# Splitting the input weights once and reading the parts back from device memory

## The chip, the cores and the metric

The kernel runs on one core of one Trainium2 chip. The core has a matrix engine (TensorE, PE in the profile, with its weight loads as PEld), three engines for elementwise work (VectorE or DVE, ScalarE or ACT, GpSimd or POOL), a queue that issues all of this kernel's transfers (SyncE or SP), and 16 DMA engines that move the bytes between device memory and the on-chip buffers. The metric is the device time of one execution in microseconds; less is better.

## The reference: one step of a streaming encoder layer

The input is 2048 new frames of one stream (1024 wide), 16 learned meta tokens ahead of them, and 32 further frames of a second, running stream with a cache of 16 + 512 keys and values. In short:

```
n = rmsnorm(x, norm_g)                       # 1024 wide
q, k, v, z_a, b, c, u, z_c = split(n @ w_in) # w_in is 1024 x 4096, eight parts of 512
for 4 heads (q, k in two halves of 64):      # keys visible up to the query's chunk of 64
    a = softmax(q1 k1/8 + bias) - lambda * softmax(q2 k2/8 + bias)
    o = 0.8 * rmsnorm(a @ v, subln_g) * silu(z_a)
y_c = silu(z_c) * b * conv3(c * u)           # causal, depthwise, width 3
y = rmsnorm(x + concat(o, y_c) @ w_out)
```

Outputs are y for both streams, the new keys and values, and the last two rows of the convolution's input. Everything is float32.

## The kernel before

**Products in three parts.** TensorE is fed with numbers of a rounded float32 kind (F32R). To keep float32's accuracy each operand is cut in two: a high part, which is the operand rounded by a cast, and a low part, which is the operand minus the high part. A product is then three: high x high, high x low, low x high. In `proj` these are the three matmuls of line 212 for each of eight slices of the 1024 inputs.

**Blocks and units.** The new frames go in four blocks of 512 tokens (`p` = 0 to 3); block 0 also carries the meta tokens and the 32 frames of the second stream, 560 columns in all. The normalised input of a block stays on chip, transposed, as eight pairs of high and low slices (`xh`, `xl`, from `x_load`). For each block the loop at line 725 goes over four heads. `unit_a(h, p)` projects keys, values, queries and gate of one head: four tiles of 128 columns of `w_in`. `attend` scores the queries against all keys so far (lines 428 and 429, 16 to 2064 of them), takes the softmax of both halves (lines 375 to 383) and multiplies with the values (lines 444 to 461). `unit_c(u, p)` does one 128-channel tile of the convolution: four more tiles of `w_in`. So each block goes through all 32 column tiles of `w_in`, 128 tile visits in all. Afterwards lines 740 to 743 do the output projection (line 676) and the final norm for 17 tiles of tokens.

**A weight tile.** `w_load(col, p)` brings one tile of 128 columns (1024 x 128, 512 KB) into a staging tile `wr`, of which there are two. It then handles it in two halves of 512 inputs: ScalarE casts the half to its high part `wh` (line 191), and GpSimd, or VectorE for a few tiles, subtracts to get the low part `wl` (line 192). There are four buffers for `wh` and four for `wl`, so two whole tiles can stand ready. In block 0 each matmul group runs twice, over two column ranges of about 280 tokens; in later blocks once, over 512: 48 and 24 matmuls for a tile. The same 32 tiles are loaded and cut again in each of the four blocks.

**Keys and queries around an attention.** The scores need the high part of a half head's keys in partitions 0 to 63 and the low part in 64 to 127. So the parts of new keys (`kh`, `kl`, lines 235 and 236) and queries (`qh`, `ql`, lines 313 and 314) are moved across partitions by transfers: eight for q, four for new ks. Earlier keys and values are kept in device memory (`ksd`, `vd`) and read back in each later block: four transfers for ks, two for v. There is one buffer of `ks` and of `q`, so these transfers start when the attention before has read its own. The bias tile `bz` has one buffer too.

**What sets the order.** The program names engines and tiles; a planner with a simulated clock puts all instructions of an engine in one order at build time, and each engine, and SP with the transfers, keeps that order at run time. A buffer is handed on when every instruction that reads it has ended. All transfers go through SP (the helper at line 73), so one that must wait holds those behind it.

**The output projection's input.** `load_cat` (line 643) reads a tile of the concatenated result into the same staging buffers as `wr` and cuts it in two into the same buffers as `wh` and `wl`.

Of the kernel before, what the change touches and what calls it, by code (L numbers as in the profile page):

```python
# [11 lines left out]
F32 = mybir.dt.float32  # L12
F32R = mybir.dt.float32r
AF = mybir.ActivationFunctionType
ALU = mybir.AluOpType
AX = mybir.AxisListType

P = 128
D = 1024
KT = D // P  # L20
# [9 lines left out]
EPS = 1e-6  # L30
# [17 lines left out]
def hybrid_step(ctx: ExitStack, tc: tile.TileContext, x, xT, ckT, cv, scT, rel_bias, norm_g, w_in,  # L48
# [28 lines left out]

# [1 line left out]
    ident = const.tile([P, P], F32, name="ident")  # L79
# [16 lines left out]

# [1 line left out]
    xh, xl = {}, {}  # L98
    rbs = {}

    def x_stats(p):
        """1 / rms of each token, in the token's partition."""
        ssq = sm.tile([P, 8], F32, tag="ssq", name="ssq", bufs=1)
        for j in range(8):
            xr = one.tile([P, QT], F32, tag="xt", name="xr", bufs=XB)
            r0 = NX + QT * p + P * (j // 2)
            dma(xr, x[r0:r0 + P, 512 * (j % 2):512 * (j % 2) + 512])
            S.activation(xr, xr, AF.Square, accum_out=ssq[:, j:j + 1])
        ssp, var, r, w = (sm.tile([P, 4], F32, tag=f"x{i}", name=f"x{i}", bufs=1) for i in range(4))
        V.tensor_reduce(ssp, ssq.rearrange("p (t i) -> p t i", i=2), op=ALU.add, axis=AX.X)  # L110
        rsqrt(r, ssp, var, w, 1.0 / D)
        return r

    def x_rms(p, r):
        """rb[:, t] = 1 / rms of token t, the same in every partition."""
        rb = one.tile([P, NX + QT], F32, tag="rb", name="rb")
        pb = ps_j.tile([P, 512], F32, tag="pj", name="pb")
        dg = one.tile([P, QT], F32, tag="xt", name="dg", bufs=XB)
        with tc.high_priority():
            V.tensor_tensor(by_tile(dg), ident.unsqueeze(1).broadcast_to([P, 4, P]),  # L120
                            r.unsqueeze(2).broadcast_to([P, 4, P]), op=ALU.mult)
            T.matmul(pb, lhsT=ones, rhs=dg, start=True, stop=True)
            S.copy(rb[:, :QT], pb)
        rbs[p] = rb
# [38 lines left out]
    def rsqrt(r, ssum, var, w, scale):  # L163
        """r = 1/sqrt(scale * ssum + EPS), with one Newton step on the table's value."""
        V.tensor_scalar(var, ssum, scale, EPS, op0=ALU.mult, op1=ALU.add)
        S.activation(r, var, AF.Ln)
        S.activation(r, r, AF.Exp, scale=-0.5)
        V.tensor_tensor(w, r, r, op=ALU.mult)
        V.tensor_tensor(w, w, var, op=ALU.mult)
        V.tensor_scalar(w, w, -0.5, 1.5, op0=ALU.mult, op1=ALU.add)  # L170
        V.tensor_tensor(r, r, w, op=ALU.mult)

    def softplus_neg(out, z):
        """log(1 + exp(-z)) for any z: beyond 40 it equals -z in float32."""
        V.tensor_scalar(out, z, -1.0, 40.0, op0=ALU.mult, op1=ALU.min)
        S.activation(out, out, AF.Exp)
        S.activation(out, out, AF.Ln, bias=1.0)
        V.scalar_tensor_tensor(out, z, -1.0, out, op0=ALU.mult, op1=ALU.max)

# [1 line left out]
    pre = {}  # L181

    def w_load(col, p):
        wr = wp.tile([P, KT, P], F32, tag="wraw", name="wr")
        dma(wr, w_in[col])
        w2 = []
        for i in range(2):
            wh = wp.tile([P, KT // 2, P], F32R, tag="wh", name="wh", bufs=4)
            wl = wp.tile([P, KT // 2, P], F32R, tag="wl", name="wl", bufs=4)
            wi = wr[:, KT // 2 * i:KT // 2 * (i + 1)]  # L190
            S.copy(wh, wi)  # L191
            (V if (col in (CK, CV) if p == 0 else col in (CQ, CZ)) else G).tensor_tensor(wl, wi, f32(wh), op=ALU.subtract)  # L192
            w2.append((wh, wl))
        return w2
# [20 lines left out]

# [1 line left out]
    ksd = [dram.tile([2, P, NK], F32, name=f"ksd{h}", tag=f"ksd{h}") for h in range(H)]  # L217
# [121 lines left out]

# [1 line left out]
    def coefs(nm, l, nch, pn, lam=None):  # L341
        """nm, l: [pn, components, nch] negated maxima and sums; returns the factor of each (component, chunk)."""
        n = nm.shape[1]
# [18 lines left out]
    def softmax_diff(pn, chunks, mm, bz):  # L362
        """chunks: [(first column, width)]; mm(c, ps, col, w) writes negated scores, bz is the negated bias of the
        last 512 columns; returns the chunks of a."""
        nch = len(chunks)
# [20 lines left out]
    def chunks_of(t):  # L386
        """The columns (16 meta, then t + 1 tiles of 128) in pieces of at most 512, cut between tiles."""
        n = t + 1
        g = -(-(NM + P * n) // 512)
        cuts = [n * j // g for j in range(g + 1)]  # L390
        cols = [0] + [NM + P * c for c in cuts[1:]]
        return [(cols[j], cols[j + 1] - cols[j]) for j in range(g)]
# [73 lines left out]
    def attend_sample(h, st):  # L466
        """Rows 0..31: component 0 of the queries; rows 32..63: component 1."""
        kts, cvt, q2, (z32, l1) = st["kts"], st["cvt"], st["qs"], st["z"]
# [38 lines left out]

# [1 line left out]
    def unit_c(u, p):  # L509
# [54 lines left out]

# [1 line left out]
    bvs, bzd = [], []  # L566
# [22 lines left out]
    def prep_small():  # L589
# [18 lines left out]
        S.activation(ls, ls, AF.Exp)  # L608
        # (1, -lambda) / sg and EPS / sg^2 with sg = max(1, |lambda|): the head norm keeps its value, and its range.
        sg = const.tile([P, 2], F32, name="sg")  # L610
# [11 lines left out]

# [1 line left out]
    y0 = [dram.tile([P, 512], F32, name=f"y0_{t}", tag=f"y0_{t}") for t in range(17)]  # L624
# [18 lines left out]
    def load_cat(t, rows, spare=False):  # L643
# [3 lines left out]
        for i in range(2):  # L647
            c = ct[:, 4 * i:4 * i + 4, :rows]
            if spare:
                chh, cll = [pp.tile([P, 4, P], F32R, tag="p0", name="cs", bufs=NP[0]) for _ in range(2)]  # L650
            else:
                chh = wp.tile([P, 4, P], F32R, tag="wh", name="chh", bufs=4)
                cll = wp.tile([P, 4, P], F32R, tag="wl", name="cll", bufs=4) if t < 16 else chh
            S.copy(chh[:, :, :rows], c)  # L654
# [6 lines left out]
    def half_product(y, c, w, rows, ssq):  # L661
        """y (the residual) += cat @ w for 512 columns, and the sum of its squares."""
        chh, cll = c
# [52 lines left out]

# [1 line left out]
    after = (((0,), (1,), (2, 3), ()), ((0,), (1,), (2,), (3,)))  # L718
# [74 lines left out]
```

## Time and profile before

| | |
|---|---|
| Time, median of 3 runs | 1342.75 us (1339.35 to 1343.84) |
| Profiled execution, its span from first to last instruction | 1338.5 us |
| TensorE matmuls busy | 1285.5 us, 96% of the span |
| VectorE, ScalarE, GpSimd busy | 999.3, 717.6, 682.8 us |
| DMA: bytes, mean rate | 215.59 MB, 161 GB/s |
| Weight loads from `w_in` | 128 of 512 KB |

The profile is of one execution, and its times are in us from the first instruction. "Busy" is the time in which an engine's own instructions run; matmuls are pipelined, so a busy TensorE is not one at its peak. A row of a group reads: line, engine, operation, out<-in, shapes, count, busy us, mean ns of one, then the engine's idle time just before these instructions and what ended it. A row of waits reads: who waited, for whom, us in total, how often, the longest. In the table by stage each row has the stretch, its length, then busy us and count for PE, PEld, DVE, ACT and POOL, the granted TensorE clock, the share of the 16 DMA engines and GB/s. The time of a transfer to its landing runs from its issue on SP.

### The profile page before, as it was taken

Reading aid. Unit: us, or ns where it says so; the run is one execution under the profiler, and the core shown is the slowest. Engines: PE = TensorE matmul, PEld = TensorE weight load, DVE = VectorE, ACT = ScalarE, POOL = GpSimd, SP = SyncE. Lnnn points to the kernel's source line nnn. Section 1 sums busy time; section 2 is a strip of 40 time slices with the busy share of each in tenths; the row PEclk is TensorE's granted clock in tenths of the full one; section 3 lists DMA queues with packets and bytes.
Section 4 is the critical chain, followed back from the end, with each engine's and each line's share of the span. In section 5 each row is a group of like instructions: output and inputs, shape, how many; then the busy total and the mean of one; then the engine's idle time right before and its main releaser. Section 6 shows DMA issues by size and latency. Waiting matters only on the chain.

```text
span 1338.5 us, 21190 instructions
## 1 busy us (share of the span) xinstructions
PE 1285.5 (96%) x7058; PEld 1104.2 (82%) x7058; DVE 999.3 (75%) x2086; ACT 717.6 (54%) x1814; POOL 682.8 (51%) x619
## 2 busy tenths in 40 slices
PE   8899999999999999999999999998999999999997
PEld 6899999977878878878878788887887877878875
DVE  8677676668887958788888898786785895777753
ACT  5554454555564547454645566465554665674432
POOL 4555556455555663565566535564574573452200
PEclk9999999999999999999999999999999999999999
DMA  8754543894445377545453463636247348445851
GB/s 276 229 155 125 164 117 104 245 274 138 139 147 158 103 209 232 141 151 150 150 135 126 120 208 93 167 124 143 94 110 203 117 160 215 165 150 185 273 196 52
DMA packets 118670, 215.59 MB, mean 161 GB/s; under 512 B 19840, under 2 KB 48032, under 8 KB 118560
## 3 DMA queue, kind: packets, MB, share of 16 engines
q1 hardware_dynamic: 118560, 214.23, 54.7%
q8 instruction: 56, 0.92, 0.3%
q14 instruction: 54, 0.44, 0.1%
HBM read 145.62 MB, written 43.26 MB: 141 GB/s over the span
## 4 chain that ended last, share of the span: by engine, by line
PE 59%; DVE 16%; DMA 10%; issue 4%; ACT 4%; POOL 3%; SPq 2%; DVEq 0%; POOLq 0%; ACTq 0%
PE pj L212 37%; PE po L676 6%; DVE p L383 3%; PE s L428 3%; DMA q<-r 3%; PE s L429 3%; PE pt L444 3%; SPq L73 2%; DVE nm L378 2%; PE po L452 2%; PE po L453 2%; PE po L451 2%; DMA ks<-ksd 1%; ACT p L379 1%; POOL wl L192 1%
## 5 line engine op out<-in xcount | busy, mean ns | idle before, releaser
L212 PE MATMUL pj<-xh,wh 128*128 128x512 f32 (+2 forms) x1280 | 457.0, 358 | 4.0 <-ACT wh L191 1.3
L192 POOL TENSOR_TENSOR wl<-wr,wh 128x512 fp32r<-128x512 f32 x240 | 328.7, 1375 | 250.2 <-ACT wh L191 234.7
L212 PE MATMUL pj<-xl,wh 128*128 128x512 f32 (+2 forms) x1280 | 455.1, 356 | 0.8 <-DVE xl L140 0.8
L212 PE MATMUL pj<-xh,wl 128*128 128x512 f32 (+2 forms) x1280 | 454.7, 356 | 0.0
L379 ACT ACTIVATE p<-s,nm 128x384 f32<-128x384 f32 (+5 forms) x352 | 208.8, 595 | 186.8 <-DVE nm L378 135.1
L212 PEld LDWEIGHTS pj<-xh,wh 128*128 128x128 f32 x1280 | 243.2, 190 | 34.2 <-ACT bvec L586 2.0
L212 PEld LDWEIGHTS pj<-xh,wl 128*128 128x128 f32 x1280 | 242.9, 190 | 31.2 <-issue 1.3
L212 PEld LDWEIGHTS pj<-xl,wh 128*128 128x128 f32 x1280 | 243.4, 190 | 30.1 <-DVE xl L140 1.4
L191 ACT CAST wh<-wr 128x512 fp32r<-128x512 f32 x256 | 157.0, 616 | 129.4 <-PE pj L212 78.6
L383 DVE SCALAR_TENSOR_TENSOR p<-p,cf,p 128x384 f32<-128x384 f32 (+5 forms) x176 | 174.5, 1019 | 28.1 <-POOL p L382 27.8
L428 PE MATMUL s<-ks,q 128*128 128x384 f32 (+5 forms) x352 | 129.5, 375 | 26.8 <-DMA q<-r 10.0
L382 POOL TENSOR_SCALAR p<-p,cf 128x384 f32<-128x384 f32 (+5 forms) x176 | 125.0, 726 | 49.2 <-DVE cf L359 35.1
L378 DVE TENSOR_REDUCE nm<-s 128x1 f32<-128x400 f32 (+3 forms) x224 | 122.5, 557 | 28.2 <-PE s L429 27.9
L429 PE MATMUL s<-ks,q 128*128 128x384 f32 (+5 forms) x352 | 124.0, 354 | 2.0 <-DMA q<-r 2.0
L448 DVE TENSOR_TENSOR al<-pt,ah 128x512 fp32r<-128x512 f32 x144 | 97.0, 682 | 37.0 <-ACT ah L447 36.9
L656 POOL TENSOR_TENSOR cll<-ct,chh 128x512 fp32r<-128x512 f32 x40 | 53.9, 1353 | 113.6 <-ACT chh L654 105.4
L428 PEld LDWEIGHTS s<-ks,q 128*128 128x128 f32 x352 | 66.2, 190 | 42.5 <-issue 14.4
L447 ACT CAST ah<-pt 128x512 fp32r<-128x512 f32 x144 | 79.1, 585 | 40.8 <-PE pt L444 40.7
L375 DVE CUSTOM_DVE_ANT_0 s<-s,bz 128x512 f32<-128x512 f32 (+5 forms) x128 | 74.4, 585 | 17.9 <-PE s L429 13.5
L444 PE MATMUL pt<-ident,p 128*128 128x128 f32 x544 | 86.5, 274 | 0.0
L452 PE MATMUL po<-al,vh 128*128 128x256 f32 x288 | 84.2, 292 | 1.9 <-DVE al L448 1.7
L451 PE MATMUL po<-ah,vh 128*128 128x256 f32 x288 | 81.6, 283 | 0.0
(243 smaller groups left out, 2138.4 us busy)
## 6 DMA issues: line engine op xcount, KB each, us to landing
wr<-in_w_in SPq DMA_DIRECT2D x128, 512.0 KB, 4.1
q<-r SPq DMA_DIRECT2D x128, 128.0 KB, 4.7
ct<-cat SPq DMA_DIRECT2D x28, 512.0 KB, 4.8
out<-y SPq DMA_DIRECT2D x32, 256.0 KB, 3.4
ks<-ksd SPq DMA_DIRECT2D x16, 388.0 KB, 7.8
xr<-in_x SPq DMA_DIRECT2D x24, 256.0 KB, 4.8
out<-g SPq DMA_DIRECT2D x24, 256.0 KB, 4.5
xt<-in_xT SPq DMA_DIRECT2D x24, 256.0 KB, 4.2
```

Source lines behind the costliest of these rows:

```text
L191: S.copy(wh, wi)
L192: (V if (col in (CK, CV) if p == 0 else col in (CQ, CZ)) else G).tensor_tensor(wl, wi, f32(wh), op=ALU.subtract)
L212: T.matmul(ps, lhsT=a[:, k % 4], rhs=b[k][:, b0:b1], start=(k == 0 and i == 0), stop=(k == KT - 1 and i == 2))
L378: V.tensor_reduce(nm[:, c, j:j + 1], s, op=ALU.min, axis=AX.X)
L379: S.activation(pr[j][c], s, AF.Exp, bias=nm[:, c, j:j + 1], scale=-1.0, accum_out=l[:, c, j:j + 1])
L382: G.tensor_scalar(a0, a0, cf[:, 0, j:j + 1], 1.0, op0=ALU.mult, op1=ALU.mult)
L383: V.scalar_tensor_tensor(a0, a1, cf[:, 1, j:j + 1], a0, op0=ALU.mult, op1=ALU.add)
L428: T.matmul(ps, lhsT=qd[c][0][:, qs], rhs=ks[c][:, col:col + w], start=True, stop=False)
L429: T.matmul(ps, lhsT=qd[c][1][:, qs], rhs=ks[c][:, col:col + w], start=False, stop=True)
L444: T.transpose(pt[:, i, P * qi:P * (qi + 1)], cols(aa[qi], NM + P * (2 * j + i), P), ident)
L451: T.matmul(po, lhsT=vh[:, kt], rhs=ah[:, i], start=(kt == 0), stop=False)
L452: T.matmul(po, lhsT=vh[:, kt], rhs=al[:, i], start=False, stop=False)
```

## The change

In block 0 a weight tile is loaded and cut as before, but the two parts of a half lie side by side in one buffer (`w2`, four buffers of twice the size), and each half is also stored to device memory, high and low part together, 512 KB a half. In blocks 1 to 3 nothing is staged or cut: each half comes with one load of 512 KB from there straight into a `w2` buffer, two loads for a tile where there was one. The choice of VectorE or GpSimd for the subtraction is that of block 0. `load_cat` takes its two parts from one `w2` buffer. Comments and docstrings are taken out as well; they are left out here.

```diff
+    wd = [dram.tile([P, 2, 2, KT // 2, P], F32, name=f"wd{c}", tag=f"wd{c}") for c in range(32)]
+
     def w_load(col, p):
-        wr = wp.tile([P, KT, P], F32, tag="wraw", name="wr")
-        dma(wr, w_in[col])
+
+        if p == 0:
+            wr = wp.tile([P, KT, P], F32, tag="wraw", name="wr")
+            dma(wr, w_in[col])
         w2 = []
         for i in range(2):
-            wh = wp.tile([P, KT // 2, P], F32R, tag="wh", name="wh", bufs=4)
-            wl = wp.tile([P, KT // 2, P], F32R, tag="wl", name="wl", bufs=4)
-            wi = wr[:, KT // 2 * i:KT // 2 * (i + 1)]
-            S.copy(wh, wi)
-            (V if (col in (CK, CV) if p == 0 else col in (CQ, CZ)) else G).tensor_tensor(wl, wi, f32(wh), op=ALU.subtract)
+            w = wp.tile([P, 2, KT // 2, P], F32R, tag="w2", name="w2", bufs=4)
+            wh, wl = w[:, 0], w[:, 1]
+            if p == 0:
+                wi = wr[:, KT // 2 * i:KT // 2 * (i + 1)]
+                S.copy(wh, wi)
+                (V if col in (CK, CV) else G).tensor_tensor(wl, wi, f32(wh), op=ALU.subtract)
+                dma(wd[col][:, i], w)
+            else:
+                dma(w, wd[col][:, i])
             w2.append((wh, wl))
         return w2
...
             else:
-                chh = wp.tile([P, 4, P], F32R, tag="wh", name="chh", bufs=4)
-                cll = wp.tile([P, 4, P], F32R, tag="wl", name="cll", bufs=4) if t < 16 else chh
+                w = wp.tile([P, 2, 4, P], F32R, tag="w2", name="cw2", bufs=4)
+                chh, cll = w[:, 0], w[:, 1] if t < 16 else w[:, 0]
```

## The prediction, made before the change was run

> **What bounds the kernel now.** I read the page's header first, then the busy time by stage, then what TensorE waited for in the three later token blocks, then one of those waits in the chain, and last what the DMA queue did around it. The header:
>
> ```profile
> span 1338.5 us, 21190 instructions
> PE 1285.5 (96%) x7058; PEld 1104.2 (82%) x7058; DVE 999.3 (75%) x2086; ACT 717.6 (54%) x1814; POOL 682.8 (51%) x619
> ```
>
> The same by stage. The first block (p = 0) ends near 250 us, the last projection near 1075 us; the columns are busy time with the number of instructions, granted clock, share of the DMA engines, GB/s:
>
> ```profile
> 0.00:50.00 50.00, 42.31 (x249) 37.11 (x250) 35.68 (x76) 25.50 (x54) 22.51 (x28) 1.00 0.85 259
> 50.00:250.00 200.00, 197.73 (x1526) 191.53 (x1525) 132.16 (x334) 98.22 (x260) 116.56 (x117) 1.00 0.54 149
> 250.00:300.00 50.00, 49.84 (x257) 41.06 (x256) 36.22 (x82) 32.21 (x82) 23.45 (x21) 1.00 0.91 274
> 300.00:500.00 200.00, 195.48 (x981) 162.75 (x979) 159.22 (x324) 108.47 (x267) 119.03 (x104) 0.99 0.51 148
> 500.00:700.00 200.00, 192.11 (x966) 162.18 (x966) 160.54 (x323) 113.61 (x292) 107.56 (x96) 0.98 0.56 159
> 700.00:900.00 200.00, 195.98 (x1009) 165.44 (x1010) 167.75 (x312) 117.67 (x290) 109.63 (x96) 1.00 0.49 144
> 900.00:1075.00 175.00, 166.88 (x880) 143.17 (x880) 131.69 (x256) 96.89 (x241) 96.20 (x83) 0.98 0.50 135
> ```
>
> TensorE sets the end nearly everywhere. From 250 to 1075 us, the only stretch where work is removed, it is busy 800.3 of 825 us: 24.7 us are idle. The granted clock of 0.98 to 0.99 in three of these rows is worth 0.01 x 200 + 0.02 x 200 + 0.02 x 175 = 9.5 us more. So **34 us is the most that any relief of the other engines can give**. What ended TensorE's waits in that stretch (total us, times, longest):
>
> ```profile
> PE s L428 <- DMA q<-r: 6.8, 5, 2.7
> PE s L428 <- DMA bz<-bz: 4.9, 1, 4.9
> PE s L428 <- ACT p L379: 4.7, 8, 1.0
> PE s L428 <- DMA ks<-r: 2.5, 1, 2.5
> ```
>
> Three of the four are transfers at the head of an attention; no row of that list has L212 waiting for weights. Why they are late shows in the chain (start, us, what) and in the DMA queue (SP) over the same time:
>
> ```profile
> 538.32 1.75 POOL wl L192
> 540.07 0.02 issue
> 540.09 5.32 DMA wr<-in_w_in
> ...
> 545.93 7.31 DMA ks<-r
> ```
>
> ```profile
> 540.09 0.33 SPq L73 DMA_DIRECT2D wr<-in_w_in  x1
> 540.50 0.47 SPq L73 DMA_DIRECT2D q<-r  x1
> 541.02 0.59 SPq L73 DMA_DIRECT2D ks<-ksd  x1
> ...
> 547.17 5.77 SPq L73 DMA_DIRECT2D q<-r  x7
> 553.30 0.33 SPq L73 DMA_DIRECT2D bz<-bz  x1
> 553.82 0.33 SPq L73 DMA_DIRECT2D wr<-in_w_in  x1
> ```
>
> SP takes its transfers in order. A weight load that waits for POOL's subtraction of an older tile (its staging buffer comes free then) stood ahead of the q and ks transfers, which then ran as a **train** of 13 us.
>
> **The change, part by part.**
>
> *Removed in the blocks p = 1 to 3* (96 of 128 weight tiles): the cast and the subtraction of each half tile.
>
> ```profile
> L192 POOL TENSOR_TENSOR wl<-wr,wh 128x512 fp32r<-128x512 f32 x240 | 328.7, 1375 | 250.2 <-ACT wh L191 234.7 <-ACT nm L354 6.3 <-PE pj L212 4.4
> L191 ACT CAST wh<-wr 128x512 fp32r<-128x512 f32 x256 | 157.0, 616 | 129.4 <-PE pj L212 78.6 <-DMA wr<-in_w_in 24.0 <-POOL p L382 7.2
> L192 DVE TENSOR_TENSOR wl<-wr,wh 128x512 fp32r<-128x512 f32 x16 | 11.7, 743 | 6.6 <-ACT wh L191 6.6
> SPq L73 <- POOL wl L192: 373.6, 84, 14.2
> ```
>
> ACT loses 192 x 0.616 = 118 us, POOL 180 x 1.375 = 247 us, DVE 12 x 0.743 = 9 us. All of it lies beside TensorE's 97%, so its direct worth is nothing. Indirectly SP no longer stands behind POOL (373.6 us of its waits by the last row, all blocks), ql and kl do not queue behind a subtraction, and exponentials do not queue behind a cast. DVE gains as well: the same tiny instruction (2 columns) takes 0.15 us or 1.28 us, the softmax difference between 0.36 and 1.78 us (least, median, most):
>
> ```profile
> L358 DVE TENSOR_TENSOR r<-r,lam x52: 147/161/1282, 70.6 to 1204.9; 128x2 f32<-128x2 f32 x52
> L383 DVE SCALAR_TENSOR_TENSOR p<-p,cf,p x176: 360/935/1783, 61.0 to 1209.6; 128x384 f32<-128x384 f32 x64, 128x400 f32<-128x400 f32 x44, 128x512 f32<-128x512 f32 x44, 128x272 f32<-128x272 f32 x16
> ```
>
> [...]
>
> Bounds of the relief: 0 (the late transfers are late for the transfers' own sake) and -34 us. The chain above and the ACT row (4.7 us) speak for POOL and ACT, the bz row and the length of the train for the transfers; I take half of the ceiling, **-16 us**.
>
> *Added in p = 0*: 64 stores of 512 KB, 33.6 MB, each issued by SP behind its subtraction. Their price in DMA time is bounded by two rates: 274 / 0.91 = 301 GB/s from the busiest row above, and the best 1.25 us slice of that stretch, 393 GB/s:
>
> ```profile
> GB/s 288 208 210 197 200 329 280 244 377 393 306 308 205 118 319 256 328 382 311 306 290 333 208 304 333 332 325 213 225 208 254 375 323 334 113 318 203 323 303 56
> ```
>
> ```profile
> DMA packets 118670, 215.59 MB, mean 161 GB/s; under 512 B 19840, under 2 KB 48032, under 8 KB 118560
> ```
>
> That is 85 to 111 us of all engines, or 0.34 to 0.45 of 250 us, on top of (50 x 0.85 + 200 x 0.54) / 250 = 0.60: 0.94 to 1.05. The stores wait behind nothing that TensorE needs and have the rest of a column's stay in the ring to finish, but they share the queue with loads that it needs. In the first 50 us some ten stores (13 to 17 us of DMA) meet 0.85: 6 to 10 us too much. The block's other 200 us have room by the lower price. Bounds 0 (loads go first) and +20 us (startup's 10, and 0.05 x 200 = 10); I take the lower overload, **+6 us**. If the ring were held up by a store, TensorE would wait its landing; the ring's two tiles last 2 x 250 / 32 = 15.6 us, so I cost that at nothing.
>
> *Moved in p = 1 to 3*: the load. Before, one load of 512 KB goes to a staging tile, is cut, and the parts wait in their own ring. After, two loads of 512 KB go straight into the ring of 4 half tiles, so a load can be issued only when TensorE has finished the same half two tiles earlier. What waits in front of it on SP now delays TensorE, and what queues behind it waits for TensorE. The cost sits at the trains. Three of them, all of TensorE's work first, then the projection (L212) alone:
>
> ```profile
> 540.50:553.80 13.30, 10.87 (x55) 8.77 (x53) 10.76 (x22) 6.28 (x17) 7.31 (x8) 1.00 0.98 211
> 686.00:699.20 13.20, 11.96 (x60) 9.80 (x58) 11.59 (x24) 5.94 (x16) 10.25 (x10) 1.00 0.98 212
> 919.50:934.70 15.20, 13.69 (x64) 10.76 (x62) 7.91 (x21) 9.18 (x22) 5.22 (x4) 1.00 0.94 210
> 540.50:553.80 13.30, 10.25 (x40) 6.91 (x38) 1.00 0.98 211
> 686.00:699.20 13.20, 10.86 (x45) 7.89 (x43) 1.00 0.98 212
> 919.50:934.70 15.20, 12.18 (x49) 8.90 (x49) 1.00 0.94 210
> ```
>
> The DMA engines are 94 to 98% busy for the whole train, and TensorE uses it to run 134 projection matmuls in 41.7 us, 0.311 us each: 24 make a column tile, so 7.5 us per tile. The ring holds 48 at best and 36 (one half empty) at worst, 15.0 or 11.2 us; when no load goes out inside the 13.2 us train, the next half tile arrives a landing after it:
>
> ```profile
> wr<-in_w_in SPq DMA_DIRECT2D x128, 512.0 KB, 4.1
> ```
>
> With 0.33 us of issue that is at 17.6 us: TensorE stands 2.6 to 6.4 us, middle 4.5. One us of it TensorE loses there already (13.3 - 10.9, 13.2 - 12.0, 15.2 - 13.7 are 1.2 to 2.4). So 3.5 us a train. There are 12 attentions in the three blocks; in five of them the q transfers go out apart from the ks ones, as here, with a load just ahead:
>
> ```profile
> 772.09 5.43 SPq L73 DMA_DIRECT2D q<-r  x8
> ```
>
> so seven full trains: **+24 us**. Bounds: 0 (loads go out ahead of or inside each train, and cost nothing) and 12 x 6.4 = 77 us. Loads inside a train that is 98% full push its q transfers back instead, so the planner can only choose who is late. Between the trains the window from release to use is 1.5 tiles, 11 us, against 4.4: hidden, with 7 us of cover. The 160 further issues at 0.33 us are 53 us of a queue that idles between trains; in a train they are in the sum above.
>
> [...]
>
> *Renamed*: the parts of the output projection's input use the new ring. Its size per partition is the same (4 x 4 KB for 4 x 2 and 4 x 2), the staging tiles are free earlier. Cost nothing; bounds -5 and +5 us, of the 17.8 us that TensorE idles there (263.0 - 245.2):
>
> ```profile
> 1075.00:1338.00 263.00, 245.18 (x1198) 200.99 (x1196) 176.01 (x383) 125.07 (x330) 87.83 (x78) 0.98 0.54 173
> ```
>
> **Sum.** Against the profiled span: 1338.5 - 16 + 6 + 24 = 1352.5. The runs' median, 1342.75, lies 4.25 above it; I carry half of that, since the runs reach down to 1339.35: **1354 us**, 0.8% slower.
>
> **The rivals.**
>
> *Faster: relief without late weights.* The planner puts each load ahead of the train or between its transfers, and POOL, DVE and ACT catch up so far that q and ks come in time: the ceiling of 34 less the 6 of the stores, from 1342.75, gives 1315 in full and 1329 with 20 of the 34. For it: the chain's step from POOL's subtraction to SP. Against: trains at 98% need no POOL to be long. It decides as soon as loads inside a train cost under 16 / 12 = 1.3 us each attention.
>
> *No change.* TensorE's idle time is the transfers' own, weights stay hidden and the stores as well: 1343. For it: 97% busy. Against: 33.6 MB stored and 96 x 512 KB = 50.3 MB loaded more, on the 215.59 MB of the row above.
>
> *Late weights everywhere.* Loads queue behind all twelve attentions at 4.5 us, with only 8 us of relief: 1342.75 - 8 + 6 + 54 = 1395.
>
> *Stores choke the first block.* Overload of 20 us, its upper bound, with the startup and the loads of the next block's x at 250 us (0.91 already) late, while trains cost half: 1342.75 - 16 + 20 + 12 = 1359.
>
> **How the numbers follow.** A measurement tells about 0.3% (4 us) from no change. Forecast 0.37, its own range 1341 to 1368; faster rival 0.29; no change 0.13; late weights 0.12; choked first block 0.09. Faster: 0.29 and 0.01 of the forecast's lower end, 0.30. Same: 0.13 and 0.03 of it, 0.16. Slower: the rest, 0.54. For 8 in 10 the range reaches to the middle of the faster rival, 1324, and to the lower part of the late weights, 1388.
>
> **What would show it.** Right, step by step: ACT near 600 us and POOL near 436, DVE below 985; SP's waits for POOL's subtraction confined to the first 250 us; DMA share about 0.94 or more in 50 to 250 us; a new row, L212 waiting for a weight load, of 20 us or more, right behind trains. Wrong: that row missing or below 8 us (then the ring is deep enough and the faster rival holds), TensorE's waits at L428 unchanged (then they were never POOL's), or a first block that ends later than 260 us (then the stores decide).

## Result and profile after

The changed kernel takes **1373.98 us** (median of 4 runs, 1372.79 to 1375.71) against 1342.62 (1339.35 to 1343.84) for the kernel before on the same chip: ratio 1.0234, 95% interval 1.0216 to 1.0252. It is 31 us slower, where 14 us over the profiled span, 1354 in all, were forecast.

The page's header of the changed kernel:

```profile
span 1373.1 us, 20932 instructions
...
PE 1300.5 (95%) x7058; PEld 1114.7 (81%) x7058; DVE 900.1 (66%) x2074; ACT 621.8 (45%) x1622; POOL 433.4 (32%) x439
```

The relief came as announced: ScalarE 622, GpSimd 433, VectorE 900 us. The same 7058 matmuls run; TensorE's busy time grew by 15.0 us (1300.5 - 1285.5), and its idle time from 53.0 to 72.6 us. So of 34.6 us of longer span **19.6 are standing time and 15.0 are the same matmuls running slower**. By stage (length, then busy us and count for PE, PEld, DVE, ACT, POOL, granted clock, DMA share, GB/s):

```profile
0.00:50.00 50.00, 42.49 (x252) 37.15 (x253) 33.83 (x76) 24.96 (x52) 22.72 (x28) 1.00 0.91 295
50.00:250.00 200.00, 189.87 (x1416) 181.31 (x1415) 129.80 (x326) 93.14 (x251) 109.29 (x110) 0.97 0.88 282
250.00:300.00 50.00, 46.51 (x273) 39.63 (x272) 21.58 (x64) 23.14 (x65) 11.79 (x13) 0.97 0.93 291
300.00:500.00 200.00, 192.28 (x969) 161.94 (x968) 126.44 (x329) 77.53 (x213) 46.86 (x50) 0.98 0.72 220
500.00:700.00 200.00, 192.72 (x972) 162.26 (x971) 137.43 (x322) 97.64 (x257) 50.64 (x54) 0.98 0.78 232
```

In the first block, where TensorE stood 2.3 of 200 us before, it now stands 10.1 at a clock of 0.97, and 110 matmuls fewer are run (1416 against 1526). From 300 to 500 and from 500 to 700 us the DMA share rose from 0.51 and 0.56 to 0.72 and 0.78, and the clock is no higher (0.98 twice, 0.99 and 0.98 before), although three engines have far less to do.

TensorE's waits after the first block, 250 to 1103 us (total us, times, longest), and then SP's largest waits over the whole run:

```profile
PE s L436 <- DMA q<-r: 12.3, 10, 2.8
PE pj L220 <- DMA w<-wd: 9.5, 3, 6.2
PE s L437 <- DMA q<-r: 5.1, 11, 1.0
PE s L436 <- DMA w<-wd: 3.2, 1, 3.2
```

```profile
SPq L73 <- PE pj L220: 366.5, 131, 6.7
SPq L73 <- POOL w L197: 70.3, 34, 7.1
```

SP no longer stands behind GpSimd (70 us in place of 374); it now stands behind the projection, whose tiles set the ring free. The forecast row, L220 waiting for weights, is there with 9.5 us, less than the 20 foreseen. The waits of the scores for q are larger, 12.3 and 5.1 us for the first and the second matmul of a pair, but before they were 6.8 us (L428) and this:

```profile
PE s L429 <- DMA q<-r: 1.4, 4, 0.6
```

So the waits for q grew by 9.2 us and those of the projection for weights, from nothing, by 9.5 (one wait of the scores, 3.2 us, also ended with a weight load). One wait for q in SP's order, in the chain that ended it, and on TensorE (start, duration, what):

```profile
514.45 0.60 SPq L73 DMA_DIRECT2D w<-wd  x1
515.91 0.56 SPq L73 DMA_DIRECT2D cat<-o  x1
517.02 0.32 SPq L73 DMA_DIRECT2D w<-wd  x1
518.98 6.68 SPq L73 DMA_DIRECT2D q<-r  x8
```

```profile
518.35 0.61 ACT r L321
...
522.08 5.31 DMA q<-r
```

```profile
526.13 0.39 PE L436 MATMUL s<-ks,q 128*128 128x272 f32 x1 [2.75 <-DMA q<-r]
```

The weights are in time, and q is late. The weight loads stand ahead of q in SP's order, but here they did not hold it back: the last is issued by 517.3 us, and SP then waits 1.6 us until ScalarE's cast of q (L321) has ended. The transfers then take 5.3 us to land; the median of all q transfers is 5.2 us (4.7 before).

### The profile page after: what moved, and what is told of

Its sections match the earlier page's. It is cut to its first block, busy times and chain, and to the rows that moved or that the text cites. A ratio compares the mean times of both kernels' runs of the same rounds, so it can differ in the third digit from the quotient of the medians.

```text
span 1373.1 us, 20932 instructions
## 1 busy us (share of the span) xinstructions
PE 1300.5 (95%) x7058; PEld 1114.7 (81%) x7058; DVE 900.1 (66%) x2074; ACT 621.8 (45%) x1622; POOL 433.4 (32%) x439
## 4 chain that ended last, share of the span: by engine, by line
PE 41%; DMA 11%; DVE 6%; ACT 2%; SPq 2%; issue 1%; POOL 0%; DVEq 0%; ACTq 0%
PE pj L220 21%; PE po L684 6%; PE s L436 3%; PE s L437 3%; DMA q<-r 3%; PE pt L452 3%; DMA ks<-ksd 2%; PE po L460 2%; SPq L73 2%; PE po L461 2%; PE po L459 2%; DMA ct<-cat 2%; DMA w<-wd 1%; DVE p L391 1%; DMA ks<-r 1%
## 5 line engine op out<-in xcount | busy, mean ns | idle before, releaser
L220 PE MATMUL pj<-xh,w 128*128 128x512 f32 (+2 forms) x2560 | 717.1, 360 | 12.2 <-DMA w<-wd 9.5
L220 PEld LDWEIGHTS pj<-xh,w 128*128 128x128 f32 x2560 | 457.5, 192 | 77.4 <-issue 7.9
L220 PE MATMUL pj<-xl,w 128*128 128x512 f32 (+2 forms) x1280 | 458.4, 358 | 1.1 <-DVE xl L140 1.1
L220 PEld LDWEIGHTS pj<-xl,w 128*128 128x128 f32 x1280 | 245.7, 192 | 31.5 <-DVE xl L140 1.8
L391 DVE SCALAR_TENSOR_TENSOR p<-p,cf,p 128x384 f32<-128x384 f32 (+5 forms) x176 | 148.9, 874 | 24.0 <-POOL p L390 23.8
L436 PEld LDWEIGHTS s<-ks,q 128*128 128x128 f32 x352 | 67.8, 195 | 45.7 <-DMA q<-r 14.3
L197 POOL TENSOR_TENSOR w<-wr,w 128x512 fp32r<-128x512 f32 x60 | 80.6, 1352 | 54.8 <-ACT w L196 34.4
L664 POOL TENSOR_TENSOR cw<-ct,cw 128x512 fp32r<-128x512 f32 x40 | 53.9, 1358 | 114.5 <-ACT cw L662 114.5
L437 PEld LDWEIGHTS s<-ks,q 128*128 128x128 f32 x352 | 68.3, 195 | 17.4 <-DMA q<-r 8.7
L461 PE MATMUL po<-ah,vl 128*128 128x256 f32 x288 | 82.0, 285 | 0.0
L452 PEld LDWEIGHTS pt<-ident,p 128*128 128x128 f32 x544 | 66.3, 142 | 6.3 <-DVE p L391 1.2
```

What stands on the lines that cost most here:

```text
L220: T.matmul(ps, lhsT=a[:, k % 4], rhs=b[k][:, b0:b1], start=(k == 0 and i == 0), stop=(k == KT - 1 and i == 2))
L391: V.scalar_tensor_tensor(a0, a1, cf[:, 1, j:j + 1], a0, op0=ALU.mult, op1=ALU.add)
L436: T.matmul(ps, lhsT=qd[c][0][:, qs], rhs=ks[c][:, col:col + w], start=True, stop=False)
L437: T.matmul(ps, lhsT=qd[c][1][:, qs], rhs=ks[c][:, col:col + w], start=False, stop=True)
L452: T.transpose(pt[:, i, P * qi:P * (qi + 1)], cols(aa[qi], NM + P * (2 * j + i), P), ident)
L461: T.matmul(po, lhsT=vl[:, kt], rhs=ah[:, i], start=False, stop=False)
```

## The experiments

Each kernel ran beside the kernel before on the same chip (medians there 1342.4 to 1343.9 us). "Ratio" is always to that kernel. Differences of ratios below are turned into us with 1342.6; each carries about 3 to 6 us. Every kernel also gets an order of its own from the planner, which none of these runs holds fixed. A cut of code shows the edit against the change, or against the kernel that the text names.

| run | median us | ratio [95%] |
|---|---|---|
| the change | 1373.98 | 1.0234 [1.0216, 1.0252] |
| ring only | 1338.88 | 0.9958 [0.9937, 0.9979] |
| stores only | 1357.98 | 1.0111 [1.0084, 1.0138] |
| loads, no stores | 1357.73 | 1.0126 [1.0084, 1.0167] |
| half loads | 1345.41 | 1.0021 [1.0002, 1.0040] |
| no subtraction | 1329.18 | 0.9888 [0.9860, 0.9917] |
| half stores | 1347.97 | 1.0029 [1.0009, 1.0048] |
| stores from ScalarE's queue | 1361.24 | 1.0142 [1.0111, 1.0174] |
| half loads, deep ring | 1328.92 | 0.9896 [0.9871, 0.9920] |
| half loads from GpSimd's queue | 1353.02 | 1.0081 [1.0051, 1.0111] |
| full loads from GpSimd's queue | 1387.54 | 1.0340 [1.0301, 1.0380] |
| stores, bias tile first | 1354.22 | 1.0093 [1.0073, 1.0112] |
| the change, bias tile first | 1376.60 | 1.0249 [1.0228, 1.0271] |
| stores without the first ten | 1347.10 | 1.0024 [1.0009, 1.0039] |
| the first ten stores alone | 1349.39 | 1.0045 [1.0027, 1.0062] |
| the change, first five tiles stored a block later | 1362.18 | 1.0138 [1.0112, 1.0164] |

### The parts by themselves

**Ring only.** Both parts of a half in one `w2` buffer; load, cast and subtraction in all four blocks as before.

```diff
-            if p == 0:
-                wi = wr[:, KT // 2 * i:KT // 2 * (i + 1)]
...
-                dma(wd[col][:, i], w)
-            else:
-                dma(w, wd[col][:, i])
+            wi = wr[:, KT // 2 * i:KT // 2 * (i + 1)]
+            S.copy(wh, wi)
+            (V if (col in (CK, CV) if p == 0 else col in (CQ, CZ)) else G).tensor_tensor(wl, wi, f32(wh), op=ALU.subtract)
```

> Every block stages and cuts its tiles as in the kernel before; only the two parts of a half share one buffer of a ring of four, as in the changed kernel. Nothing is stored or read back. Theory A (the stores of block 0 cost the time) and theory B (the doubled loads into a ring of two tiles cost it): 1343 us, within 5, since both need traffic that is not here. Rival C (the planner's new order by itself, or the shared release of the two parts, costs it): 1355 us or more.

It is 0.4% (5.6 us) faster than the kernel before, and of the complete kernels the fastest. The renaming, costed at nothing, is no loss. Since only the shared buffers and the planner's order differ, it also shows how much these alone can move the time.

**Stores only.** The ring-only kernel with the 64 stores added; nothing reads them.

```diff
+            if p == 0:
+                dma(wd[col][:, i], w)
```

> The ring of the kernel just named and the 64 stores of block 0; blocks 1 to 3 still load, stage and cut, and nobody reads what was stored. Theory A: block 0 ends 13 us late as in the changed kernel, the start of block 1 loses a part of its 17 us, so 1358 to 1374 us. Theory B: 1343 to 1350 us.

1.0111 against 0.9958: the stores cost 1.53%, **20.5 us**, at the upper bound of the prediction and three times its value.

**Loads, no stores.** The changed kernel with one tile stored and that tile read in its place in the later blocks.

```diff
-                dma(wd[col][:, i], w)
+                if col == CK:
+                    dma(wd1[:, i], w)
...
-                dma(w, wd[col][:, i])
+                dma(w, wd1[:, i])
```

> The changed kernel with only the first tile's two halves stored; blocks 1 to 3 load every tile with two loads of 512 KB from that one stored tile, so their numbers are computed with the first tile's weights in place of the right ones. 62 of the 64 stores are left out, everything else is as in the changed kernel. Theory A: block 0 ends with the kernel before, at 254 us, and the whole is 1335 to 1350 us. Theory B: 1360 to 1374 us.

The change less this run is 1.08%, so the stores cost **14.5 us** in place. That may be too little: the two stores that remain are the first of all, and from 50 to 250 us this kernel runs 1494 matmuls against 1521 in ring only. The run itself lies between the ranges of both theories, 1.3% slower than before although the cuts are gone: the loads lose more than the relief gives. That all loads read one tile did not make them quicker; they land in 4.7 us, as in the change.

**Half loads.** As the last, but only the high part is loaded, 256 KB a half tile, and used for both.

```diff
-                dma(w, wd1[:, i])
+                dma(wh, wd1[:, i, 0])
+                wl = wh
```

> As the one without the 62 stores, but blocks 1 to 3 load only the high part of a half (256 KB, so the bytes of the kernel before) and use it in place of the low part too, which leaves the low part out of their numbers. Casts and subtractions are gone, the loads still wait for the ring. If the doubled bytes of the loads cost time (theory B by bytes), this is 10 us or more faster than the one with full loads and near 1325 us, the relief alone; if the wait for the ring costs it (theory B by depth), the two are within 5 us; under theory A within 5 us too, both below 1345 us.

With the bytes of before (2 x 256 KB a tile) the loss shrinks by 1.05%, 14.1 us. What is left is no gain, so the relief is still eaten by something that is not bytes.

### The relief

**No subtraction.** The ring-only kernel without the subtraction in blocks 1 to 3 (the high part stands for the low one); the cast stays.

```diff
-                wi = wr[:, KT // 2 * i:KT // 2 * (i + 1)]
-                S.copy(wh, wi)
-                (V if col in (CK, CV) else G).tensor_tensor(wl, wi, f32(wh), op=ALU.subtract)
+            wi = wr[:, KT // 2 * i:KT // 2 * (i + 1)]
+            S.copy(wh, wi)
+            if p == 0:
+                (V if col in (CK, CV) else G).tensor_tensor(wl, wi, f32(wh), op=ALU.subtract)
+            else:
+                wl = wh
```

> The kernel with only the shared ring (1339 us), loads, staging and casts kept in every block, but in blocks 1 to 3 no subtraction: the high part is used in place of the low part, which leaves the low parts out of these blocks' numbers. POOL loses 247 us and DVE becomes faster; the ring and the traffic are unchanged. If the relief is worth the 16 us of the prediction (and something else ate it in the changed kernel): 1322 to 1330 us. If TensorE's waits were never POOL's and DVE's: 1336 to 1342 us.

0.70% below ring only, **9.4 us**. The busy times of the two, ring only first:

```profile
PE 1286.4 (96%) x7058; PEld 1104.4 (83%) x7058; DVE 1000.4 (75%) x2086; ACT 719.4 (54%) x1814; POOL 685.4 (51%) x619
```

```profile
PE 1277.3 (97%) x7058; PEld 1099.6 (83%) x7058; DVE 915.1 (69%) x2074; ACT 723.2 (55%) x1814; POOL 433.2 (33%) x439
```

GpSimd loses 252 us, and VectorE 85 us with 12 instructions fewer (9 us by the row of before): its other instructions run shorter beside an idler GpSimd (33% busy in place of 51%). The softmax difference (lines 384 and 387), for one, takes 815 ns in place of 940 at the median. Why they do, no run here shows. TensorE is busy 9 us less as well: its mean granted clock is 0.994 against 0.988.

### The loads: depth and bytes

**Half loads, deep ring.** The same bytes as half loads, but each half tile goes to one of the two rings of before, four buffers each: four tiles stand ready in place of two. (The high part serves as the low one in blocks 1 to 3.)

```diff
+        if p > 0:
+            for i, tag in enumerate(("wh", "wl")):
+                wh = wp.tile([P, KT // 2, P], F32R, tag=tag, name="wh", bufs=4)
+                dma(wh, wd1[:, i])
+                w2.append((wh, wh))
+            return w2
```

> As the kernel that loads only high parts in blocks 1 to 3 and uses them for both (1345 us), but with the two rings of the kernel before, four buffers each, and the first half of a tile in one and the second in the other: four tiles deep in place of two, at the same bytes. The low parts are left out of these blocks' numbers. If the ring's depth (loads that can go out only just in time) cost the 6 us above the shared ring alone and ate the relief: 1323 to 1338 us. If depth is nothing and the relief is nothing: 1339 to 1346 us.

0.9896: against the kernel before, with loads of the same bytes and no cuts, **the relief gives 14.0 us**. Against half loads the two further tiles are worth 1.25%, **16.8 us**. The stretch from 300 to 1050 us, deep first, then two tiles deep, then the full loads:

```profile
300.00:1050.00 750.00, 739.37 (x3836) 629.38 (x3834) 520.85 (x1196) 343.82 (x901) 194.52 (x207) 1.00 0.52 152
```

```profile
300.00:1050.00 750.00, 731.94 (x3753) 620.42 (x3753) 514.24 (x1177) 335.07 (x882) 189.90 (x201) 0.99 0.54 150
```

```profile
300.00:1050.00 750.00, 722.78 (x3673) 610.09 (x3672) 505.16 (x1152) 328.28 (x859) 184.71 (x198) 0.99 0.69 211
```

TensorE does 83 matmuls less with two tiles ready, and 80 less again with the double bytes; at 750 / 3836 = 0.196 us apiece these are 16 us each. Standing time explains 7.4 and 9.2 of them (750 less the busy time); for the rest, the matmuls ran slower. The profiled executions of half and full loads are 2.9 us apart (spans 1348.9 and 1351.8), the medians 12.3, so the price of the bytes rests on the medians. TensorE's waits over the whole run with two tiles, with four, and with the full loads:

```profile
PE s L438 <- DMA q<-r: 13.4, 11, 2.7
PE s L439 <- DMA q<-r: 5.9, 11, 1.1
...
PE pj L222 <- DMA w<-wd: 2.4, 3, 1.4
```

```profile
PE s L438 <- DMA q<-r: 10.2, 8, 5.5
...
PE s L439 <- DMA q<-r: 2.3, 6, 0.6
```

```profile
PE s L437 <- DMA q<-r: 14.2, 12, 2.4
...
PE pj L221 <- DMA w<-wd: 8.2, 5, 2.7
PE s L438 <- DMA q<-r: 5.0, 10, 0.8
```

Less depth makes TensorE wait longer for q (from 12.5 to 19.3 us) and little for weights (2.4 us, no such row with four tiles). The double bytes add waits for weights (8.2 us) and none for q (19.2). How long SP stands for the projection is no measure of the cost: 325 us with four tiles, 358 with two.

**Loads from GpSimd's queue**, half and full. If SP's order (a load that must wait for TensorE holds q back) were the cause, another queue would cure it.

```diff
-                dma(wh, wd1[:, i, 0])
+                nc.gpsimd.dma_start(f32(wh), wd1[:, i, 0])
```

> As the kernel that loads only high parts into the ring of two tiles and uses them for both (1345 us; the low parts are left out of the later blocks' numbers), but its weight loads of blocks 1 to 3 are issued from GpSimd's queue in place of SP's, so no other transfer stands behind a load that waits for TensorE, and no load stands behind a train. If the cost of the shallow ring (16 us against the ring of four tiles) is this order on SP: 1328 to 1336 us. If it is that a load can only start when TensorE has freed a half, whoever issues it: 1342 to 1350 us; more if GpSimd's own work holds the loads up.

> As the kernel with full loads and without 62 of the 64 stores (1358 us; the later blocks' numbers use the first tile's weights), with the loads issued from GpSimd's queue. If SP's order costs the shallow ring its 16 us: 1340 to 1346 us, the doubled bytes' 12 us remaining. If not: 1354 to 1362 us.

Both are slower than with SP's queue, 1.0081 against 1.0021 and 1.0340 against 1.0126, and slower than the range of either theory. With the full loads the q transfers land in 7.6 us (5.3 with SP's queue):

```profile
q<-r SPq DMA_DIRECT2D x128, 128.0 KB, 7.6
```

So this gives no sign that SP's order makes the price of two tiles. But a load on GpSimd's queue also holds up GpSimd's own work. With the half loads its issues keep it busy for 107 us, and it stands 356 us ahead of them until the projection has freed a half:

```profile
L201 POOL DMA_DIRECT2D w<-wd x192 | 107.0, 557 | 397.3 <-PE pj L222 356.2 <-DVE pt L449 9.2 <-DVE cf L369 9.1
```

So this test is not clean; by which way a shallow ring makes q late stays open.

### The stores: the place more than the bytes

**Half stores** (the high part alone, 256 KB) and **stores from ScalarE's queue**:

```diff
-                dma(wd[col][:, i], w)
+                dma(wd[col][:, i, 0], wh)
```

```diff
-                dma(wd[col][:, i], w)
+                nc.scalar.dma_start(f32(wd[col][:, i]), f32(w))
```

> As the kernel with only the stores (1358 us, 19 above the shared ring alone), but each of the 64 stores takes the high part only, 256 KB: the same number of issues, half the bytes; nobody reads them. If the DMA engines' time in block 0 is what the stores cost (share 0.60 and 0.17 to 0.22 instead of 0.94 to 1.05, so under the limit): 1339 to 1346 us. If it is proportional to bytes: 1348 us. If the cost is SP's, by issues and waits in order: 1354 to 1360 us.

> As the kernel with only the stores (1358 us), but the 64 stores are issued from ScalarE's queue in place of SP's. If the DMA engines' time is the cost: 1354 to 1362 us again. If it is the order on SP (a store waits for its subtraction and holds the transfers behind it): 1339 to 1345 us.

Half the bytes cost 0.71%, 9.5 us, about half of 20.5, which looks like a price by the byte. Another queue changes nothing for the better: 1361 us against 1358. But the stages of the half stores speak against a price by the byte. From 50 to 250 us 76 matmuls are missing (1445 against 1521 in ring only); spread evenly, 19 of them would be missing by 100 us. The half stores from 50 to 100 us:

```profile
50.00:100.00 50.00, 43.16 (x300) 39.94 (x301) 34.39 (x89) 25.46 (x71) 26.16 (x27) 0.93 0.78 238
```

Ring only has 365 there (its row stands below), so 65 of the 76 are lost in this quarter of the stage, and 11 behind it. Stores only, with all the bytes, loses 61 there and 42 behind. (A count compares the same work only roughly, since each kernel has its own order.) Fewer bytes help the later part and not the early one. What the first attention waited for, in the changed kernel: VectorE, then TensorE behind it (start, duration, idle time):

```profile
DVE s L383 <- DMA bz<-bz: 7.6, 1, 7.6
```

```profile
60.51 0.59 PE L436 MATMUL s<-ks,q 128*128 128x272 f32 x1 [4.36 <-ACT p L387]
```

The transfer of the bias tile `bz`, which ring only issues at 31.1 us, goes out at 54.8 (53.9 in stores only), behind two stores. That gave the next theory.

**Bias tile first**, on the stores-only kernel and on the change:

```diff
+    bz = one.tile([P, 512], F32, tag="bz", name="bz", bufs=1)
+    dma(bz, bzd[0])
     for p in range(NQ):
...
-            st["bz"] = one.tile([P, 512], F32, tag="bz", name="bz", bufs=1)
-            dma(st["bz"], bzd[h])
+            if p or h:
+                bz = one.tile([P, 512], F32, tag="bz", name="bz", bufs=1)
+                dma(bz, bzd[h])
+            st["bz"] = bz
```

> The stores-only kernel, with head 0's bias tile of the first block read back before the loop over the blocks in program order, so that its transfer goes out ahead of the first q transfers and not behind two stores; all 64 stores as they were. Theory A (a good part of the stores' cost is one place: in the stores-only kernel the bias transfer is issued at 53.94 us instead of 31.11, the scores of the first attention stand 4.6 us for it, and the clock is at 0.50 to 0.53 for the next 10 us; 70 of the 103 matmuls that are missing in 50 to 250 us are missing by 100 us, about 9 us): 1349, with 360 or more matmuls in 50 to 100 us in place of 304. Theory B (the cost goes with the bytes, spread over the block): 1356 to 1358, the matmuls missing somewhere else.

> The changed kernel, complete, with the same earlier read of head 0's bias tile. Theory A: 1374 - 9 = 1365. Theory B: 1372 to 1374.

The theory fell: the long wait is gone, but 290 matmuls are run in 50 to 100 us, not 360, and the times are 1354 (stores only 1358, a difference within the noise) and 1377 (the change 1374). The stage was still late. So the next two kernels split the stores themselves.

**Without the first ten, and the first ten alone.** The first five weight tiles: in the change six of their ten stores go out by 33 us, the other four from 53.7 to 57.5 us.

```diff
-            if p == 0:
+            if p == 0 and col not in (CQ, CK, CV, CZ, CC):
                 dma(wd[col][:, i], w)
```

```diff
-            if p == 0:
+            if p == 0 and col in (CQ, CK, CV, CZ, CC):
                 dma(wd[col][:, i], w)
```

> The stores-only kernel without the stores of the first five weight tiles, that is, 10 of the 64 stores (16% of the bytes) left out: those that are issued before 70 us, ahead of and around the first attention. Theory C (the place decides: the stores that meet the start, whose transfers already fill the DMA engines, make the first attention late and halve the clock there, about 9 of the 20 us): 1350, with 350 or more matmuls in 50 to 100 us. Theory B (the cost goes with the bytes over the whole block): 1355.

> The complement: the ring-only kernel with the stores of the first five weight tiles alone, 10 of 64. Theory C: 1348, with about 305 matmuls in 50 to 100 us as in the stores-only kernel. Theory B: 1342 (0.16 of the 20 us).

Ten stores alone cost 0.87%, **11.7 us**; the other 54 cost 0.66%, 8.9 us. Together that is the 20.5 of all 64. Here are 50 to 100 us for ring only, for the 54 late stores, and for the ten early ones:

```profile
50.00:100.00 50.00, 48.00 (x365) 45.68 (x365) 37.60 (x94) 27.66 (x78) 29.15 (x29) 1.00 0.62 172
```

```profile
50.00:100.00 50.00, 47.77 (x362) 45.49 (x363) 34.79 (x94) 27.87 (x79) 28.80 (x30) 1.00 0.90 292
```

```profile
50.00:100.00 50.00, 42.92 (x298) 39.90 (x297) 31.76 (x84) 25.41 (x71) 22.52 (x25) 0.90 0.64 197
```

With the late stores the DMA engines are 90% busy and TensorE loses 3 matmuls. With the early ones they are 64% busy and it loses 67, about 9 us (50 / 365 each): 5.1 us more standing time, and a clock of 0.90. So the share in this stretch is not what harms. With the early stores SP is later through startup and issues the q transfers at 47.2 us in place of 44.1. Here is what goes out from there on; then the next weight load in ring only, and in stores only with the bias tile first:

```profile
47.24 5.51 SPq L73 DMA_DIRECT2D q<-r  x8
52.79 1.07 SPq L73 DMA_DIRECT2D wd<-w  x2
53.90 0.96 SPq L73 DMA_DIRECT2D bz<-bz  x1
54.97 1.63 SPq L73 DMA_DIRECT2D wd<-w  x2
56.65 2.50 SPq L73 DMA_DIRECT2D wr<-in_w_in  x2
```

```profile
49.99 1.08 SPq L73 DMA_DIRECT2D wr<-in_w_in  x2
```

```profile
56.73 2.47 SPq L73 DMA_DIRECT2D wr<-in_w_in  x2
```

The longest stand of the early stores, 5.1 us, is again one for the bias tile, which goes out behind two stores (the chain that ended the stand, then TensorE):

```profile
53.90 5.19 DMA bz<-bz
```

```profile
60.17 0.59 PE L432 MATMUL s<-ks,q 128*128 128x272 f32 x1 [5.08 <-ACT p L383]
```

TensorE stood, and then ran at half clock:

```profile
55.00:60.00 5.00, 0.09 (x1) 0.00 (x0) 0.76 (x5) 0.35 (x2) 0.00 (x0) 0.62 0.96 351
60.00:65.00 5.00, 4.83 (x17) 4.10 (x18) 4.32 (x20) 4.10 (x16) 1.09 (x3) 0.50 0.99 356
```

Ring only runs 32 and 42 matmuls in these two stretches, at a clock of 1.00: the next tile's weights were issued at 50.0 us, and its projection runs between the scores. With the early stores these loads go out 6.7 us later. With the bias tile first they are as late, which may be why that kernel gained so little. But they also leave at 56.7 us when the stores are on ScalarE's queue, where no store stands ahead of them on SP, and no kernel here moves them alone. That ten stores at this place cost the time is shown; by which of the late transfers is not.

**The change with these five tiles stored a block later** (cut again in block 1, stored there, read in blocks 2 and 3), complete:

```diff
+        cut = int(col in (CQ, CK, CV, CZ, CC))
-        if p == 0:
+        if p <= cut:
...
-            if p == 0:
+            if p <= cut:
...
-                dma(wd[col][:, i], w)
+                if p == cut:
+                    dma(wd[col][:, i], w)
```

> The changed kernel, complete, with the first five weight tiles cut again in the second block and stored there, and read ready-made only in the last two. Theory C: 1366 (9 less, one more for ten halves cut once more). Theory B: 1374, since as many bytes are stored as before.

1.0138 in place of 1.0234: **12.9 us come back** with as many bytes stored. Five of the 96 tile loads of the later blocks fall away as well; at 30.9 us for all of them (16.8 + 14.1 above) that is an estimated 1.6 us of the 12.9. By the medians the place of ten stores is most of what the stores cost; it does not turn the change into a gain.

## Why the prediction was right or wrong

The direction was right, and the time lies in the wide range (1324 to 1388), though above the forecast's own (1341 to 1368). The size was wrong: 31.4 us as the difference of two medians, 14 in the sum. Of the 17.4 us between them 8.5 belong to the stores' term, 6.9 to the loads' and 2.0 to the relief's; the rest of the 20 us from 1354 to 1374 is the way from span to median. From the kernel before to the change the runs give: relief with a deep ring -14.0, two tiles of depth less (and the shared ring) +16.8, double bytes of the loads +14.1, stores +14.5, which by construction add up to +31.4.

**Bounds of the kernel, and the relief, -16: right.** -14.0 where the loads hurt nobody; -9.4 for the subtraction alone. The figure was half of a ceiling, chosen and not worked out, so that it came so near is partly luck. The way named (GpSimd no longer in front of SP, VectorE below 985) is in the rows: 70 us of SP's waits, VectorE 900.

**The stores, +6: the step that failed.** "I take the lower overload" counted only DMA time beyond full engines. They cost 14.5 in place and 20.5 alone. The *place* of the 6 us was nearly right: of the "some ten stores" in the first 50 us six go out by then and four just behind. These ten cost 11.7, with a late first attention: alone, they bring 5.1 us more standing time from 50 to 100 us and a clock of 0.90 there. The other 54, "room by the lower price" and so nothing, cost 8.9. And the measure itself was wrong: from 50 to 100 us 3 matmuls were lost at a share of 0.90 and 67 at 0.64, where transfers that TensorE needed had gone out late. The share announced, 0.94 or more, was 0.88. The sentence "a first block that ends later than 260 us (then the stores decide)" came true. Its projection, alone, up to 268.0 us and up to 254.4 us, after, and before:

```profile
0.00:268.00 268.00, 217.65 (x1536) 204.74 (x1536) 0.97 0.89 285
```

```profile
0.00:254.40 254.40, 204.31 (x1435) 191.99 (x1436) 0.97 0.88 283
```

```profile
0.00:254.40 254.40, 215.33 (x1536) 203.93 (x1536) 1.00 0.61 172
```

All 1536 matmuls were started by 254.4 us before; 101 were still missing then after the change.

**The loads, +24: near in size, half right in kind.** 30.9 us (16.8 + 14.1), inside 0 to 77. The lack of depth was the right cause, worth 16.8 us even at the bytes of before. But I let TensorE stand for weights alone (20 us or more; 9.5 measured, between the two signs that I had set) and named the other way, "push its q transfers back instead", only as the planner's choice; the waits for q grew by as much, 9.2 us. The doubled bytes, 14.1 us, had no term of their own between the trains ("hidden, with 7 us of cover"). The "one us" that TensorE loses in a train already is 1.2 to 2.4 by its own three figures; their mean of 1.7 would have made the term about 19.

**A cost left out of every added term: the clock.** The ceiling of the relief contained it, the losses didn't. Standing time grew by 19.6 us and slower matmuls took 15.0 more. Here it went with the stands and not with the DMA share: from 50 to 100 us the clock was 1.00 at a share of 0.90 with 2.2 us of standing time (the late stores), and 0.90 at 0.64 with 7.1 us (the early ones).

**The rivals.** The faster one needed loads that cost nothing; that held only with the deep ring at half the bytes (1329, its very number, but for another kernel). "Stores choke the first block" (1359) had the right place, startup, and 20 us for the stores, near the 20.5 of the stores alone, though by the same measure of full engines; and it halved the loads, which it should not have. "Late weights everywhere" (1395) gave the loads 54 us, where 30.9 were measured. "No change" fell with both, the stores and the loads.

## What to carry to other kernels

Work taken off engines that are not the bound is worth what it held up, here 14 us for some 350 us of engine time removed (96 on ScalarE, 249 on GpSimd, 9 on VectorE); and it must not be paid for in bytes (here 14.1 us for the doubled loads) nor with the depth of a ring (16.8 us for two tiles). A store that nobody waits for is not free in startup, where ten cost 11.7 us here: ask what lands later because of it, not whether the DMA engines have room, and put it a stage later. To every us that TensorE will stand add the clock that it may lose afterwards, in this case three quarters as much again (15.0 us of slower matmuls beside 19.6 us more standing time).

## What was not expected

**Short stands and the clock.** In the changed kernel TensorE stood 2.75 us up to 526.13 us, ran one matmul of 0.39 us, and stood again:

```profile
527.52 0.36 PE L437 MATMUL s<-ks,q 128*128 128x272 f32 x1 [1.00 <-DMA q<-r]
```

```profile
523.00:526.13 3.13, 0.38 (x2) 0.00 (x1) 0.69 (x1) 0.59 (x1) 0.00 (x0) 1.00 0.87 194
527.10:528.10 1.00, 0.58 (x3) 0.57 (x4) 0.18 (x1) 0.00 (x0) 0.00 (x0) 1.00 0.95 291
528.10:529.00 0.90, 0.90 (x4) 0.68 (x3) 0.59 (x2) 0.61 (x3) 0.00 (x0) 0.56 1.06 335
```

The granted clock is 1.00 up to 528.1 us and 0.56 behind it, when TensorE had work again. The two stands before it are 2.75 and 1.00 us, 3.75 together. That they brought the lower clock is the author's reading of this order; no run here varies a stand by itself.

**Loads issued by GpSimd.** With the same bytes they cost 8.0 us more (half loads, 1.0081 - 1.0021) and 28.7 us more (full loads, 1.0340 - 1.0126) than from SP's queue. Why so much more is open.
